# Pairing the short TensorE pieces of two recurrences in one decoder layer

## The chip, the core and the metric

The kernel is one program on one core of a Trainium2 chip. Its time is the device time of one launch, in microseconds (us). TensorE multiplies matrices; its matrix instructions come from one in-order stream. VectorE (DVE), ScalarE (ACT) and GpSimd (POOL) do the elementwise work, and SyncE (SP) issues most of the transfers. All five run their own in-order streams and wait for each other through semaphores.

## The reference, cut to what matters

One layer, batch 1, 512 tokens, width 1024, everything float32:

```
h = x + 1/2 * SwiGLU_1(RMSNorm(x))
h = h + HybridMixer(RMSNorm(h))
h = h + 1/2 * SwiGLU_2(RMSNorm(h))
y = RMSNorm_final(h)
```

The mixer projects the normed input to some 13,000 columns and uses them in two branches:

```
HGRN2, 8 heads:           S = diag(f_t) S + k_t^T v_t          o_t = S^T q_t
Gated DeltaNet, 16 heads: S = a_t (I - b_t k_t k_t^T) S + b_t k_t v_t^T   o_t = S^T q_t
y = sigmoid(gate_h) * (o_hgrn W_h) + sigmoid(gate_g) * (o_gdn W_g);   return y W_out
```

Both recurrences are computed in chunks; the second needs, for each chunk and head, the inverse of a unit triangular matrix.

## The kernel before

Activations lie feature by feature: 8 tiles of 128 partitions (features) by 512 tokens. Every dense product is done in three matmuls of rounded halves (`mm3`, L165 to L168: high by high, high by low, low by high), each 128x512. A row marked L166, L167 or L168 is one of these; three of them, a *triple*, are the smallest dense step. Weights come in slabs of 128x512 that SP loads (`raw`), ACT rounds (`whi`, L2179) and DVE subtracts (`wlo`, L2181).

The three stages follow each other: the first SwiGLU, the mixer, the second SwiGLU. In the mixer, dense products (`product`, L2201) and the two recurrences share TensorE. The recurrences use plain float32 matmuls in short pieces, each a few instructions long:

- HGRN2 (`h_head`, L1274): `pd` (L1289), seven levels of `pl` (L1326 on 128x32 tiles of the array, L1340 on smaller tiles), then `po` and `pu` by chunk (L1387 to L1392).
- Gated DeltaNet works on eight pairs of heads, u = 0 to 7, in four chunks of 128 tokens. Ahead of a recurrence stand `pgq` (L1592) and the triangular inverse with `pq1` to `pq4` (L1681 to L1712, on 32x32 and 64x64 tiles). The recurrence itself (`g_rec`, L1725) is a chain by chunk: `pks` (L1766, L1767) reads the state `s`; DVE makes `x` or `gx` from it (L1770); `pw` (L1779) reads that; DVE makes `we` or `gwe` (L1784) and ACT copies `w` or `gw` (L1736); `pog` (L1793, L1795) reads these; DVE makes the next `s` (L1806). That is 3 `pks`, 4 `pw` and 4 `pog` in each of eight recurrences, 88 pieces.

The order of all five engines in the mixer is fixed while the program is built, by a planner (`Desk`, L54). Each thread of work is a generator that asks for an engine for an assumed time: 0.69 us for a dense triple, 0.46 for `pw`, 0.88 for `pks`, 0.9 for `pog`, 0.65 or 0.6 for `pq1` to `pq4`. `run` (L107) repeatedly takes the engine that can start earliest and, on it, the thread of the lowest rank that is ready. Recurrences have ranks under 9, the dense products rank 9. So a short piece goes in front of the next triple as soon as it is ready, and ready means `SLACK` = 0.8 us after its inputs are planned to be done. The instructions are issued in the planned order; on the chip only that order is kept, and semaphores set the times.

Of the kernel before, what the change touches and what calls it, by code (L numbers as in the profile page):

```python
# [19 lines left out]
D = 1024  # L20
# [25 lines left out]
STAY = (15,)  # L46
CONVS = 6
SLACK = 0.8
LAG = dict(raw=3.5, gb=6.5, nb=6, m=7, out=5, back=6)
EASE = 2.5  # L50
LANES = {"a": 2, "b": 2, "d": 1, "e": 1}
# [2 lines left out]
class Desk:  # L54
# [5 lines left out]
    def __init__(self, **places):  # L60
        self.left, self.at, self.idle, self.now = dict(places), {}, {}, 0.0
        self.busy, self.asked, self.cur = [], [], None

    def start(self, rank, gen):
        th = type("Thread", (), {})()
        th.rank, th.gen, th.t = rank, gen, self.cur.t if self.cur else self.now
        self.resume(th)
# [39 lines left out]
    def run(self):  # L107
        self.settle()
        while self.busy:
            ready = {}  # L110
            for th in self.busy:
                e = th.want[1]
                r = th.t + (SLACK if e == "PE" and th.rank[0] < 9 else 0)
                ready.setdefault(e, []).append((r, th))
            t, e = min((max(self.idle.get(e, 0.0), min(r for r, _ in w)), e) for e, w in ready.items())
            th = min((th for r, th in ready[e] if r <= t), key=lambda th: th.want[3:] or th.rank)
            self.now = t
            self.idle[e] = th.t = t + th.want[2]
            self.busy.remove(th)
            self.resume(th)  # L120
            self.settle()
        assert not self.asked, [(th.rank, th.want) for th in self.asked]


def body(tc, xT, cst, sqc, hmask, dta, w1o, w1a, w2a, wm, wt, wn, wab, wbh, wbg, wo, w1b, w2b, yT, yN, dbg=None):
# [889 lines left out]
    with tc.tile_pool(name="mp", bufs=1) as mp:  # L1015
        mixer(tc, mp, locals())
# [7 lines left out]
def mixer(tc, mp, e):  # L1024
    nc = tc.nc
    pe, act, dve, pool, sp = nc.tensor, nc.scalar, nc.vector, nc.gpsimd, nc.sync
# [9 lines left out]
    def v3(ap, a):  # L1036
        return ap.rearrange("p (a b) -> p a b", a=a)
# [18 lines left out]
    for size, names in ((1024, "n2:2 gz:2 fs:1 ut:1"), (512, "kn:3 gm:1 qm:2 gb:2 ln:1 at:4 vb:4 t64:2 on:2"),  # L1056
                        (256, "ft:1 tp:1 thg:2 x:1 we:1 s:3 w:1"), (128, "fm:1"), (64, "sm:4")):
        for it in names.split():
            n, b = it.split(":")
# [39 lines left out]
    D = Desk(xt=0, zo=0, wx0=1, wx1=1, wx2=1, wx3=1, mm=2, a=2, b=2, d=1, e=1, ta=TA, tm=6, thg=1, raw=RB, w=WB, n2=2, gz=2, fs=1, ut=1, t=3, kn=3, gm=1,  # L1099
             qm=2, gb=2, ln=1, mi=3, mt=3, at=4, vb=4, t64=2, on=2, ft=1, x=1, we=1, w_=1, s=3)  # L1100
# [15 lines left out]
    def turned(x, src, mem, then=None, *arg, step=True):  # L1116
# [7 lines left out]
        sp.dma_start(mem, x)  # L1124
        yield "lag", LAG["out"]

# [9 lines left out]
    def regroup(to, mem):  # L1136
# [4 lines left out]
        else:  # L1141
            rows = mem.rearrange("(t s) (b c r) -> c (s b) t r", t=4, b=4, c=NT)
            for c in range(NT):
                yield "use", "SP", .5
                sp.dma_start(v3(to[:, c], 4), rows[c])
        yield "lag", LAG["back"]


    def decays(pab):
# [71 lines left out]
        sp.dma_start(gtd, gt)  # L1221
        yield "lag", LAG["out"]
        D.fire("decays")
# [284 lines left out]
    def g_e(u, st):  # L1508
# [3 lines left out]
        for i in range(2):  # L1512
# [4 lines left out]
            sp.dma_start(gb, gtd[hd_:hd_ + 1].rearrange("o (c b) -> o c b", c=NT).to_broadcast([P, NT, P]))  # L1517
            yield "lag", LAG["gb"]
            a = G["at"][u % 4 * 2 + i]
# [91 lines left out]
    def g_b(u, st):  # L1611
# [4 lines left out]
        for b in range(4):  # L1616
            r = slice(32 * b, 32 * b + 32)
            yield S
            sp.dma_start(nb[b].rearrange("s i j -> i s j"), n2[r, :, :, r].rearrange("p a c j -> p (a c) j"))
        yield "lag", LAG["nb"]  # L1620
        yield "on", *([("P", u - 2)] if u > 1 else [("m2", 0)] if u else ["m"])
# [9 lines left out]
        sp.dma_start(t, eye4)  # L1631
        yield "lag", LAG["m"]
        for j in range(31):
# [665 lines left out]
    def norm():  # L2299

        acc = e["acc"]
        yield "get", "d", 1
        yield "lag", 7.6
        yield T_(1.8)
        pt = ps("pst")
        for i in range(NT):
            c = slice(i * P, (i + 1) * P)
            pe.matmul(pt[:, i:i + 1], acc[:, c], ones[:, :1], start=True, stop=False)
            pe.matmul(pt[:, i:i + 1], rbc[:, c], ones[:, :1], start=False, stop=True)
        yield V(4)  # L2310
        v = rcols[:, 4:8]
        dve.tensor_scalar(v, pt[:, :4], 1.0 / (KD * P), EPS, op0=ALU.mult, op1=ALU.add)
        D.put("d")
        yield "use", "POOL", 1.2
        pool.tensor_tensor(rcol, v, mhalf[:, :4], op=ALU.pow)
        yield "get", "d", 1
        yield T_(.9)
        pb = ps("pbc")
        for i in range(NT):
            pe.matmul(pb[:, i * P:(i + 1) * P], rcol[:, i:i + 1].to_broadcast([P, P]), ident, start=True, stop=True)  # L2320
        yield A(512)
        act.copy(rbc, pb)
        D.put("d")
        D.fire("rbc")

    G["tp"] = [places["tp"]("gtp", (P, 8, 32))]
    D.start((0,), norm())
    D.start((3, -1), loader())
# [126 lines left out]
```

## Time and profile before

| | |
|---|---|
| median of 3 runs | 1584.68 us (1583.71 to 1585.51) |
| the profiled execution | 1584.17 us, span 1582.1 us |
| TensorE busy | 1574.2 us of the span |
| VectorE busy | 1095.0 us (69%) |
| ScalarE busy | 867.2 us (55%) |
| mean granted TensorE clock | 0.999 of full speed |
| first recurrence piece of DeltaNet (`pw`) | at 731.4 us of the span |
| last of them to start (`pw`, u = 7) | at 1085.3 us |

A row of the timeline gives the start from the span's beginning, the time that the merged instructions took, engine, line, operation, what was written from what, tile of the array and shape, and how many were merged. A float32 matmul of a short piece appears as two records. Starts of TensorE's instructions are recorded, ends are modelled and overlap the next start, so costs on TensorE are read from start to start.

### The profile page before, as it was taken

How to read it: one execution, taken by the hardware profiler on the slowest of the kernel's cores; microseconds unless marked ns; L12 is line 12 of the kernel's file. 1: busy time of each engine (PE TensorE's matmuls, PEld its weight loads, DVE VectorE, ACT ScalarE, POOL GpSimd, SP SyncE). 2: the span in 40 equal slices, each digit the busy share in tenths (PEclk: the TensorE clock that was granted, in tenths of full speed). 3: DMA queues.
4: the chain of work that ended last, by engine and by line, in shares of the span. 5: the costliest groups of instructions: out<-in, count | busy, mean ns of one | idle time of the engine just before them, and what ended most of it. 6: DMA issues, size and time to landing. Idle time of an engine off the chain costs nothing.

```text
span 1582.1 us, 28663 instructions
## 1 busy us (share of the span) xinstructions
PE 1574.2 (100%) x10344; PEld 1357.7 (86%) x10344; DVE 1095.0 (69%) x2027; ACT 867.2 (55%) x1891; POOL 382.9 (24%) x727
## 2 busy tenths in 40 slices
PE   9999999999999999999999999999999999999998
PEld 8999998888788788888888888888888899999887
DVE  5988884547778668758878776564555888888352
ACT  7776663334326335657576666554234766666232
POOL 0322200100222221074550566600001322220011
PEclk9999999999999999999999999999999999999999
DMA  6888843542323224565454765565645888873342
GB/s 218 180 205 184 186 100 88 181 122 91 101 68 95 72 80 138 163 211 174 127 167 129 224 193 157 185 202 159 205 155 171 219 185 186 186 169 95 90 137 90
DMA packets 172397, 240.66 MB, mean 152 GB/s; under 512 B 40272, under 2 KB 65488, under 8 KB 172256
## 3 DMA queue, kind: packets, MB, share of 16 engines
q1 hardware_dynamic: 155408, 208.55, 41.8%
q0 software_dynamic: 16416, 29.89, 12.3%
q8 instruction: 81, 1.33, 0.3%
q14 instruction: 60, 0.49, 0.1%
q10 hardware_dynamic: 432, 0.40, 0.1%
HBM read 208.07 MB, written 30.70 MB: 151 GB/s over the span
## 4 chain that ended last, share of the span: by engine, by line
PE 96%; issue 1%; DMA 1%; DVE 1%; SPq 0%; ACT 0%; POOL 0%; POOLq 0%; DVEq 0%; ACTq 0%
PE pmm L166 19%; PE pmm L168 18%; PE pmm L167 18%; PE pfa L475 3%; PE pfy L168 2%; PE pfx L167 2%; PE pfy L166 2%; PE pfx L168 2%; PE pfy L167 2%; PE pfx L166 2%; PE pnat L166 2%; PE pfa L167 2%; PE pfa L168 2%; PE pfa L166 2%; PE pnat L168 2%; PE pnat L167 2%
## 5 line engine op out<-in xcount | busy, mean ns | idle before, releaser
L166 PE MATMUL pmm<-uhl,whi 128*128 128x512 f32 x788 | 326.2, 414 | 0.1
L168 PE MATMUL pmm<-uhl,wlo 128*128 128x512 f32 x788 | 308.4, 391 | 0.3 <-DVE wlo L162 0.3
L167 PE MATMUL pmm<-uhl,whi 128*128 128x512 f32 x788 | 307.6, 390 | 0.0
L2179 ACT CAST whi<-raw 128x512 fp32r<-128x512 f32 x230 | 142.5, 620 | 235.7 <-PE pmm L167 184.7
L2181 DVE TENSOR_TENSOR wlo<-raw,whi 128x512 fp32r<-128x512 f32 x230 | 161.3, 704 | 144.1 <-ACT whi L2179 138.2
L168 PEld LDWEIGHTS pmm<-uhl,wlo 128*128 128x128 f32 x788 | 147.9, 188 | 33.2 <-DVE wlo L162 0.7
L166 PEld LDWEIGHTS pmm<-uhl,whi 128*128 128x128 f32 x788 | 148.2, 188 | 28.9 <-DVE fa L243 0.5
L167 PEld LDWEIGHTS pmm<-uhl,whi 128*128 128x128 f32 x788 | 148.5, 188 | 26.6
L166 PE MATMUL pmm<-gh,whi 128*128 128x512 f32 (+1 forms) x374 | 141.2, 377 | 0.0
L167 PE MATMUL pmm<-gl,whi 128*128 128x512 f32 (+1 forms) x374 | 140.8, 377 | 0.0
L168 PE MATMUL pmm<-gh,wlo 128*128 128x512 f32 (+1 forms) x374 | 140.8, 377 | 0.0
L439 DVE TENSOR_TENSOR sig<-h,sig 128x1024 fp32r<-128x1024 f32 x76 | 92.8, 1221 | 58.6 <-ACT sig L437 58.6
L437 ACT CAST sig<-h 128x1024 fp32r<-128x1024 f32 x76 | 79.8, 1050 | 94.0 <-PE pfx L168 33.5
L204 POOL TENSOR_TENSOR acc<-acc,sqt 128x512 f32<-128x512 f32 x18 | 24.1, 1341 | 373.5 <-ACT sqt L202 373.4
L606 DVE TENSOR_TENSOR wlo<-raw,whi 128x512 fp32r<-128x512 f32 (+1 forms) x80 | 55.5, 698 | 81.8 <-ACT whi L604 81.7
L604 ACT CAST whi<-raw 128x512 fp32r<-128x512 f32 (+1 forms) x80 | 46.9, 588 | 94.9 <-PE pmm L167 84.8
L407 POOL DMA_DIRECT2D wlo<-w1b x60 | 52.0, 868 | 140.8 <-ACT s L495 97.9
L168 PEld LDWEIGHTS pmm<-gh,wlo 128*128 128x128 f32 x374 | 70.4, 188 | 12.9
L166 PEld LDWEIGHTS pmm<-gh,whi 128*128 128x128 f32 x374 | 70.4, 188 | 12.9
L167 PEld LDWEIGHTS pmm<-gl,whi 128*128 128x128 f32 x374 | 70.4, 188 | 12.8
L1477 DVE SCALAR_TENSOR_TENSOR cy<-pmm,cs,cy 128x511 f32<-128x511 f32 (+2 forms) x96 | 71.6, 746 | 11.0 <-ACT cy L1474 8.7
L407 POOL DMA_DIRECT2D wlo<-w1a x54 | 46.8, 867 | 126.6 <-ACT s L495 85.9
(545 smaller groups left out, 4150.1 us busy)
## 6 DMA issues: line engine op xcount, KB each, us to landing
raw<-wt SPq DMA_DIRECT2D x152, 256.0 KB
raw<-w1b SPq DMA_DIRECT2D x80, 256.0 KB
raw<-w1a SPq DMA_DIRECT2D x72, 256.0 KB
wlo<-w1b POOLq DMA_DIRECT2D x60, 256.0 KB, 5.6
wlo<-w1a POOLq DMA_DIRECT2D x54, 256.0 KB, 6.2
raw<-w2a SPq DMA_DIRECT2D x40, 256.0 KB
raw<-w2b SPq DMA_DIRECT2D x40, 256.0 KB
raw<-wn SPq DMA_DIRECT2D x32, 256.0 KB
```

What stands on the lines that cost most here:

```text
L166: pe.matmul(pt, ah, bh, start=first, stop=False, **kw)
L167: pe.matmul(pt, ah, bl, start=False, stop=False, **kw)
L168: pe.matmul(pt, al, bh, start=False, stop=last, **kw)
L407: pool.dma_start(lo, src_, accum_op=ALU.add)
L437: act.copy(hl[:, 0:2], s)
L439: dve.tensor_tensor(hl[:, 2:4], s, hl[:, 0:2].bitcast(F32), op=ALU.subtract)
L475: pe.matmul(pa.rearrange("p (x t) -> p x t", x=2), hi[:, w], x, start=first and p == 0, stop=False, skip_group_check=True)
L604: act.copy(hi[:, :n], raw[:, :n])
L606: dve.tensor_tensor(lo[:, :n], raw[:, :n], hi[:, :n].bitcast(F32), op=ALU.subtract)
L1477: dve.scalar_tensor_tensor(y[:, j:], pt[:, :T - j], wc[3 - j], y[:, j:], op0=ALU.mult, op1=ALU.add)
L2179: act.copy(hi, raw)
L2181: dve.tensor_tensor(lo, raw, hi.bitcast(F32), op=ALU.subtract)
```

## The change

The planner gets two rules, both switched on in the mixer alone (`D.paired = PAIRED`).

The first holds short pieces. While the plan's clock is between 400 and 700 us, and a dense triple stands at TensorE as well, a short piece is not placed until a second one is ready, or until the first has been ready for 8 us. The rule applies only when the last thing placed on TensorE was dense, so once a piece has been placed others may follow at once.

The second charges TensorE for a change of kind: 0.03 us is added to a short piece that follows dense work, 0.115 us to a triple that follows a short piece. This holds through the whole mixer and shifts the plan's clock for all engines.

No instruction is added or taken away; the order on the five engines changes.

```diff
@@ -46,6 +46,9 @@
 STAY = (15,)
 CONVS = 6
 SLACK = 0.8
+PAIRED = 2
+WHEN = ((400, 700, 8.0),)
+TURN = 0.03, 0.115
 LAG = dict(raw=3.5, gb=6.5, nb=6, m=7, out=5, back=6)
@@ -60,6 +63,7 @@
     def __init__(self, **places):
         self.left, self.at, self.idle, self.now = dict(places), {}, {}, 0.0
         self.busy, self.asked, self.cur = [], [], None
+        self.paired, self.short = 0.0, False
@@ -107,15 +111,24 @@
     def run(self):
         self.settle()
         while self.busy:
-            ready = {}
+            ready, held = {}, 0.0
+            wait = max([v for a, b, v in WHEN if a <= self.now < b], default=0.0) if self.paired and not self.short else 0.0
+            if wait:
+                pe = [th for th in self.busy if th.want[1] == "PE"]
+                ts = sorted(th.t for th in pe if th.rank[0] < 9)
+                if ts and len(ts) < len(pe):
+                    held = min(ts[PAIRED - 1] if ts[PAIRED - 1:] else ts[0] + wait, ts[0] + wait)
             for th in self.busy:
                 e = th.want[1]
-                r = th.t + (SLACK if e == "PE" and th.rank[0] < 9 else 0)
+                r = max(th.t, held) + SLACK if e == "PE" and th.rank[0] < 9 else th.t
                 ready.setdefault(e, []).append((r, th))
             t, e = min((max(self.idle.get(e, 0.0), min(r for r, _ in w)), e) for e, w in ready.items())
             th = min((th for r, th in ready[e] if r <= t), key=lambda th: th.want[3:] or th.rank)
             self.now = t
             self.idle[e] = th.t = t + th.want[2]
+            if e == "PE" and self.paired and (th.rank[0] < 9) != self.short:
+                self.idle[e] = th.t = th.t + TURN[self.short]
+                self.short = not self.short
             self.busy.remove(th)
@@ -2323,6 +2336,7 @@
         D.fire("rbc")
 
+    D.paired = PAIRED
     G["tp"] = [places["tp"]("gtp", (P, 8, 32))]
```

Lines of this part of the program stand 13 lower after the change, so L166 becomes L179 and L1793 becomes L1806.

Two places of TensorE's order show what moves. The first is in the middle of the DeltaNet part: in the kernel before, from one `pog` to the `pks` that reads its new state (`s_8592`). `pq3` is a piece of another pair's inverse.

```order
L1793 MATMUL pog_8588<-gwe_6494,gkn_6077 128x256
L1795 MATMUL pog_8588<-gw_6555,gat_6218 128x128
L1795 MATMUL pog_8588<-gw_6555,gat_6219 128x128
L166 MATMUL pmm_8506<-uhl_71,whi_8349 128x512
L167 MATMUL pmm_8506<-uhl_71,whi_8349 128x512
L168 MATMUL pmm_8506<-uhl_71,wlo_8348 128x512
L1704 MATMUL pq3_8606<-h_70,gn2_7245 64x64 x8
L166 MATMUL pmm_8623<-uhl_71,whi_8358 128x512
L167 MATMUL pmm_8623<-uhl_71,whi_8358 128x512
L168 MATMUL pmm_8623<-uhl_71,wlo_8357 128x512
L1766 MATMUL pks_8635<-s_8592,h_70 128x256
L1767 MATMUL pks_8635<-s_8592,h_70 128x256
```

The same step of the same recurrence on TensorE after the change (the state is `s_8582` here, and `pq4` is the next piece of that inverse):

```order
L1806 MATMUL pog_8578<-gwe_6527,gkn_6096 128x256
L1808 MATMUL pog_8578<-gw_6455,gat_6238 128x128
L1808 MATMUL pog_8578<-gw_6455,gat_6239 128x128
L1725 MATMUL pq4_8589<-acc_72,gt64_7184 64x64 x8
L179 MATMUL pmm_8555<-uhl_71,whi_8352 128x512
L180 MATMUL pmm_8555<-uhl_71,whi_8352 128x512
L181 MATMUL pmm_8555<-uhl_71,wlo_8351 128x512
L179 MATMUL pmm_8555<-uhl_71,whi_8352 128x512
L180 MATMUL pmm_8555<-uhl_71,whi_8352 128x512
L181 MATMUL pmm_8555<-uhl_71,wlo_8351 128x512
L1779 MATMUL pks_8621<-s_8582,h_70 128x256
L1780 MATMUL pks_8621<-s_8582,h_70 128x256
```

The small-tile piece has moved from between two triples to directly behind `pog`; two triples and one small piece lie between `pog` and `pks` in both.

The second place is later on TensorE, from a `pks` to the `pw` that follows it in its chain. Before the change (pair u = 6):

```order
L1766 MATMUL pks_12059<-s_12025,h_70 128x256
L1767 MATMUL pks_12059<-s_12025,h_70 128x256
L166 MATMUL pmm_12009<-uhl_71,whi_11808 128x512
L167 MATMUL pmm_12009<-uhl_71,whi_11808 128x512
L168 MATMUL pmm_12009<-uhl_71,wlo_11807 128x512
L166 MATMUL pmm_12009<-uhl_71,whi_11808 128x512
L167 MATMUL pmm_12009<-uhl_71,whi_11808 128x512
L168 MATMUL pmm_12009<-uhl_71,wlo_11807 128x512
L166 MATMUL pmm_12009<-uhl_71,whi_11808 128x512
L167 MATMUL pmm_12009<-uhl_71,whi_11808 128x512
L168 MATMUL pmm_12009<-uhl_71,wlo_11807 128x512
L1779 MATMUL pw_12082<-gx_6461,gut_6341 128x128 x2
```

And at about the same count of dense triples after it (pair u = 5, which is still running there):

```order
L1779 MATMUL pks_11948<-s_11912,h_70 128x256
L1780 MATMUL pks_11948<-s_11912,h_70 128x256
L1725 MATMUL pq4_11955<-acc_72,gt64_6952 64x64 x8
L179 MATMUL pmm_11868<-uhl_71,whi_11664 128x512
L180 MATMUL pmm_11868<-uhl_71,whi_11664 128x512
L181 MATMUL pmm_11868<-uhl_71,wlo_11663 128x512
L179 MATMUL pmm_11975<-uhl_71,whi_11715 128x512
L180 MATMUL pmm_11975<-uhl_71,whi_11715 128x512
L181 MATMUL pmm_11975<-uhl_71,wlo_11714 128x512
L1792 MATMUL pw_11987<-x7_7613,x5_7637 128x128 x2
```

Between `pks` and `pw` stood three triples; now a small-tile piece joined to `pks` and two triples stand there.

## Rows read from the trace of the kernel before

**Rows 1.** The page, part 1: busy time, share, instructions of each engine.

```profile
PE 1574.2 (100%) x10344; PEld 1357.7 (86%) x10344; DVE 1095.0 (69%) x2027; ACT 867.2 (55%) x1891; POOL 382.9 (24%) x727
```

**Rows 2.** Timeline of TensorE around one `pw` that stands alone.

```profile
740.44 0.39 PE L166 MATMUL pmm<-uhl,whi 128*128 128x512 f32 x1
...
740.89 0.39 PE L168 MATMUL pmm<-uhl,wlo 128*128 128x512 f32 x1
741.12 0.60 PE L1779 MATMUL pw<-gx,gut 128*128 128x128 f32 x4
741.48 0.48 PE L166 MATMUL pmm<-uhl,whi 128*128 128x512 f32 x1
741.79 0.40 PE L167 MATMUL pmm<-uhl,whi 128*128 128x512 f32 x1
```

**Rows 3.** Timeline of TensorE around two `pw` in a row.

```profile
763.17 0.39 PE L168 MATMUL pmm<-uhl,wlo 128*128 128x512 f32 x1
763.40 0.60 PE L1779 MATMUL pw<-gx,gut 128*128 128x128 f32 x4
763.84 0.61 PE L1779 MATMUL pw<-gvb,h 128*128 128x128 f32 x4
...
764.52 0.40 PE L167 MATMUL pmm<-uhl,whi 128*128 128x512 f32 x1
```

**Rows 4.** Timeline of TensorE around one `pq2` alone.

```profile
752.61 0.39 PE L168 MATMUL pmm<-uhl,wlo 128*128 128x512 f32 x1
752.92 0.69 PE L1691 MATMUL pq<-acc,x 32*32 32x32 f32 x32
...
753.88 0.40 PE L167 MATMUL pmm<-uhl,whi 128*128 128x512 f32 x1
```

**Rows 5.** Timeline of TensorE around one `pgq` alone.

```profile
714.42 0.39 PE L168 MATMUL pmm<-uhl,wlo 128*128 128x512 f32 x1
714.65 1.02 PE L1592 MATMUL pgq<-h 128*128 128x256 f32 x4
...
715.74 0.40 PE L167 MATMUL pmm<-uhl,whi 128*128 128x512 f32 x1
```

**Rows 6.** Timeline of TensorE around `pq2` and `pgq` in a row.

```profile
929.49 0.39 PE L168 MATMUL pmm<-uhl,wlo 128*128 128x512 f32 x1
929.80 0.69 PE L1691 MATMUL pq<-acc,gtp 32*32 32x32 f32 x32
930.43 1.13 PE L1592 MATMUL pgq<-h 128*128 128x256 f32 x4
...
931.62 0.40 PE L167 MATMUL pmm<-uhl,whi 128*128 128x512 f32 x1
```

**Rows 7.** Timeline of TensorE around one `pl` on 128x32 tiles.

```profile
395.47 0.39 PE L168 MATMUL pnat<-whi,uhl 128*128 128x512 f32 x1
395.79 0.45 PE L1326 MATMUL pl<-qp,ke 128*32 128x16 f32 x32
...
396.50 0.39 PE L167 MATMUL pnat<-wlo,uhl 128*128 128x512 f32 x1
```

**Rows 8.** Timeline of TensorE around two such `pl` in a row.

```profile
577.54 0.39 PE L168 MATMUL pnat<-whi,uhl 128*128 128x512 f32 x1
577.86 0.74 PE L1326 MATMUL pl<-qp,ke 128*32 128x16 f32 x64
...
578.86 0.39 PE L167 MATMUL pnat<-wlo,uhl 128*128 128x512 f32 x1
```

**Rows 9.** Waits of TensorE, 380 to 1145 us: total, times, longest.

```profile
PE pks L1766 <- DVE s L1806: 0.2, 1, 0.2
```

**Rows 10.** Timeline of all engines: links of one chain, 736 to 744 us.

```profile
737.24 0.59 PE L1767 MATMUL pks<-s,h 128*128 128x256 f32 x2
...
739.59 0.35 DVE L1770 SCALAR_TENSOR_TENSOR gx<-pks,sm,gvb 128x128 f32<-128x128 f32 x1
...
742.50 0.61 DVE L1784 TENSOR_SCALAR gwe<-pw,gx 128x128 f32<-128x128 f32 x2
...
743.62 0.59 PE L1793 MATMUL pog<-gwe,gkn 128*128 128x256 f32 x2
```

## The prediction

> **What bounds the kernel now.** I read the busy shares of the page first: TensorE is busy for 1574.2 of 1582.1 us, and the next engine, VectorE, for 1095.0 [rows 1]. So TensorE's stream sets the time, and only two things can move it: the work in that stream becomes shorter, or TensorE has to wait. Then I read the waits of TensorE over the mixer: the view names one, 0.2 us long [rows 9]. There is nothing to win back from waits in that stretch. What remains is the cost of TensorE's own pieces, and for that I read the timeline of TensorE from start to start, at places where a short piece stands alone between dense matmuls and at places where the old order happened to put two in a row. The reader is to see in these rows what a second piece adds behind a first.
>
> **The change part by part.** Counted in the order that TensorE gets, the mixer has 196 unbroken stretches of short pieces before and 165 after, with the same instructions. So 31 times a change from dense work to short pieces and back disappears, nearly all in the DeltaNet part. The question is what one such change costs.
>
> Dense matmuls start 0.225 us apart (740.44 to 740.89 is two of them) [rows 2]. Around a lone `pw` it takes 0.90 us from the last dense start ahead of it (740.89) to the second dense start behind it (741.79); without the piece it would be two pitches, 0.45. So the lone `pw` costs 0.45 us, both changes of kind included [rows 2]. Two `pw` in a row: 763.17 to 764.52 is 1.35, less 0.45 is 0.90 us [rows 3], twice the lone one. The second piece saved nothing. The same for pieces of unlike shape: `pq2` alone costs 1.27 - 0.45 = 0.82 us [rows 4], `pgq` alone 1.32 - 0.45 = 0.87 [rows 5], the two in a row 2.13 - 0.45 = 1.68 [rows 6], against a sum of 1.69. A join is worth 0.00 to 0.01 us.
>
> Why it looks dearer is also in [rows 2]: the first dense start behind the piece is followed by the next only 0.31 us later, 0.09 more than the pitch. But that dense matmul itself had started 0.36 us after `pw`, where four records at the 0.11 us that one costs (0.45 over 4) ask for 0.44. The extra behind the piece is the piece's own tail, which the records put into the next pitch. It is not a toll that a join avoids. I take 0.005 us a join, so 31 x 0.005 = 0.2 us less; the two ends are 0 and 31 x 0.01 = 0.3.
>
> There is one kind of join that does pay. A lone `pl` on 128x32 tiles costs 1.03 - 0.45 = 0.58 us [rows 7], two in a row 1.32 - 0.45 = 0.87 [rows 8], 0.29 less than 2 x 0.58. Here both pieces use a small tile of the array, and one entry into it and exit from it is spared. The order counts four such neighbours of `pl` pieces before and three after, since the shifted plan also reorders the HGRN2 part. That is one join lost, 0.3 us more. The joins that the change makes are of another kind: a full-array piece (`pks`, `pw`, `pog`, `pgq`) beside another or beside a small-tile `pq`. Changes of tile shape in the stream number 158 before and 159 after.
>
> The Trainium skill has a rule that fits this (TensorEngine Tiling (Array Packing), Key Properties): changing the tiling mode, not merely the tile, drains the TensorE. By that rule a stretch of full-array pieces spares no drain when joined, and a full-array piece beside a small-tile one leaves both changes of mode where they were, so the rule speaks against a gain from these joins. [Rows 6] agree (0.01 us for a mixed join) and so do [rows 7, 8] (0.29 us where one visit to the small tile is spared); by the rule alone, with 159 changes of mode for 158, the sum would be a shade above no change.
>
> Next, waits. Nothing else hides behind TensorE: on the other engines the instructions are the same, and VectorE, the busiest, has 31% of idle time over the span [rows 1]. But the order fixes how many triples stand between two links of a chain, and the new charge of 0.145 us a stretch (0.03 + 0.115) is time that the planner sees and the chip does not: its old charge of 0.46 for `pw` already covers the 0.45 measured. With 165 stretches the plan now counts 165 x 0.145 = 24 us of TensorE work that, for full-array pieces, doesn't exist. So links are planned with more time than they will have. How much is there to lose? The second `gx` starts at 739.59 and takes 0.35, so it is done at 739.94, and `pw` starts at 741.12: 1.2 us spare. `gwe` is done at 743.11 and `pog` starts at 743.62: 0.5 us spare [rows 2, 10]. One or two stretches between links take 0.15 to 0.3 us of this. Most links keep something. At the two places shown in the section on the change, the distance is about what it was: `pog` to `pks` has two triples and one small piece in both, `pks` to `pw` had 3 x 0.675 = 2.0 us and now has 2 x 0.675 + 0.82 = 2.2. A held piece also has more spare time, not less, since its inputs were ready before it was let go.
>
> If a link does run dry, what waits behind it is TensorE's whole stream, the dense triples included, so each such wait is paid in full. The trace of before can't show how many there will be. Bounds: none (the 0.2 us of [rows 9] gone as well), or a third of the 88 chain pieces, 29, each late by 0.25 us (between the 0.15 and 0.3 above, rounded up), 7 us. I take 0.5 us more than now, two or three short waits, because the spare times in [rows 2, 10] are above the erosion.
>
> The transfers and weight slabs: SP's and ACT's orders shift with the plan, but the dense triples keep their count, and slabs are made several triples ahead; I cost this at nothing, hidden by the slabs that stand ready, and if that cover went, the wait would be one conversion late, under 1 us a time.
>
> Sum, against the profiled execution's 1584.17 us (span 1582.1): -0.2 for joins, +0.3 for the lost neighbour, +0.5 for waits, 1584.8. The median of the runs is 0.5 above the profiled execution, so I forecast 1585.3 us. By bounds, the forecast's own range is from 1584.68 - 0.3 - 0.2 = 1584.2 to about 1588, a handful of waits short of the 7 us.
>
> **The rivals.**
>
> Faster: a change of kind really costs what the planner charges, 0.145 us. Then 31 x 0.145 = 4.5 us go, 1580.2 us. For it: dense after short starts 0.31 apart instead of 0.225 [rows 2]. Against it: the doubled and the mixed pieces, which should then be 0.145 below their sum and are 0.00 and 0.01 below it [rows 3, 6]. Chance 0.06.
>
> Slower, by links that run dry: the 24 us that only the plan sees come off the spare time of the DeltaNet chains, and TensorE stops in front of `pks`, `pw` or `pog`. Price at the upper bound 7 us, 1592 us; it decides from about 13 late links of 0.25 us, 3.2 us. For it: the spare time at `pog` is only 0.5 us [rows 10]. Against it: one wait so far in 88 pieces [rows 9], and a held pair has more spare time. Chance 0.12.
>
> Slower, at the end: holding delays the recurrences, and the branch product that needs their last heads waits. The last `pog` stands 11 triples ahead of that product in the order before and 5 after, 6 x 0.675 = 4 us later, 1589 us if it all shows. Against it: the last two heads are read 50 triples after the product starts, some 34 us, and their transposes still stand 21 triples (14 us) ahead of that. Chance 0.04.
>
> That the change doesn't join pieces is excluded by the order: 31 stretches fewer.
>
> **How the numbers follow.** 0.2% is 3.2 us, about what a measurement of this kernel can tell from no change, so no change means 1581.5 to 1587.9. The forecast has 0.78: it lies inside, but its upper end touches 1588, and I count 0.01 of it as slower. Faster is the first rival less the case that it comes out half as large: 0.05, and 0.01 of it stays within. Slower: 0.12 less 0.01 for a mild form, plus 0.04 and the 0.01 above, 0.16. Within: 0.79. The range from 1582.3 to 1589.0 leaves out the faster rival and the heavy end of the first slower one, together near 0.15.
>
> **What would show it.** In the profile after: a `pw` or `pks` joined to another full-array piece still costs its lone 0.45 or 0.87 us from start to start; TensorE stays near 1574 us busy; TensorE's waits in the mixer total under 2 us. I am wrong if joined pieces come out 0.1 us or more below their sum (then 1580), or if waits on `s`, `gx`, `gwe` or `gw` add up to several us in front of chain pieces, or a wait of some us stands where the branch product reads its last heads.

## The result, and the profile after

The changed kernel takes 1587.37 us (median of 21 runs, 1586.74 to 1589.05) against 1584.68 us (21 runs, 1583.67 to 1586.51). The ratio is 1.0018, 95% interval 1.0012 to 1.0024: 2.7 us slower, inside the 0.2% that I had called no change, and above the 1585.3 us forecast. The profiled execution took 1588.55 us, 4.4 us more than that of before, so the sizes below are those of one execution at the slow edge.

The first line of the page after, which answers to [rows 1] (busy time, share, instructions):

```profile
PE 1575.9 (99%) x10344; PEld 1358.7 (86%) x10344; DVE 1093.6 (69%) x2027; ACT 867.1 (55%) x1891; POOL 385.0 (24%) x727
```

TensorE is as busy as it was, within 1.7 us, while the span grew from 1582.1 to 1586.6 us: the pieces did not become cheaper, and waits came. The waits of TensorE over the mixer, which answer to [rows 9] (total, times, longest):

```profile
PE po L1402 <- DVE hs L1411: 0.7, 1, 0.7
PE pq L1725 <- POOL fm L1650: 0.5, 1, 0.5
PE pd L1302 <- DVE qq L1297: 0.5, 1, 0.5
PE pmm L179 <- DVE cy L1490: 0.5, 2, 0.3
PE pmm L180 <- DVE oh L1463: 0.2, 1, 0.2
PE po L1402 <- DVE hs L1409: 0.2, 1, 0.2
```

That is 2.6 us in six kinds of waits where one wait of 0.2 us stood. Four of the six (`po` twice, `pd`, and the products that read `oh`) belong to the HGRN2 part, where nothing is held and only the charge for a change of kind acts. None of the named waits is at `pks`, `pw` or `pog`. The view leaves out shorter ones: read from start to start, two lone `pog` cost 1.14 us in place of 0.88 (at 1034.23 and 1063.89 us), as before the change two `pks` were late by 0.46 and 0.32 us (at 801.53 and 956.92 us).

All kernels here run the same number of dense triples, so the start of the triple with the same number can be compared; by the 1000th, all kernels of the table have the same short pieces behind them. The differences from before, in us, of the last row (L168 or its successor) of the 650th triple (mixer begins), the 1000th (HGRN2 done), the 1470th and 1600th (before and after the recurrences' last heads are read) and the 2350th (last):

| kernel | 650 | 1000 | 1470 | 1600 | 2350 |
|---|---|---|---|---|---|
| the change | 0.35 | 3.68 | 3.95 | 4.48 | 4.48 |
| charge_only | 0.49 | 3.82 | 12.62 | 12.62 | 12.62 |
| hold_only | 0.46 | 0.44 | -4.52 | 3.48 | 3.48 |
| charge_early | 0.05 | 3.64 | 8.10 | 8.62 | 8.62 |
| charge_late_hold | 0.04 | 0.07 | -1.53 | 4.05 | 4.05 |

A negative number means that fewer short pieces than before are done at that triple. Of the 4.1 us that the changed kernel loses in the mixer, 3.3 are lost by the 1000th triple, and 0.8 in the DeltaNet part.

**The joined pieces.** TensorE's timeline after the change, at a `pw` joined to a `pog`, and at a `pog` joined to a `pq4`; these answer to [rows 2 to 6]:

```profile
860.05 0.40 PE L181 MATMUL pmm<-uhl,wlo 128*128 128x512 f32 x1
860.28 0.61 PE L1792 MATMUL pw<-gx,x 128*128 128x128 f32 x4
860.73 0.60 PE L1806 MATMUL pog<-x,x 128*128 128x256 f32 x2
...
861.84 0.39 PE L180 MATMUL pmm<-uhl,whi 128*128 128x512 f32 x1
```

```profile
852.23 0.39 PE L181 MATMUL pmm<-uhl,wlo 128*128 128x512 f32 x1
852.45 0.59 PE L1806 MATMUL pog<-gwe,gkn 128*128 128x256 f32 x2
...
853.42 0.68 PE L1725 MATMUL pq<-acc,gt 64*64 64x64 f32 x16
...
854.37 0.39 PE L180 MATMUL pmm<-uhl,whi 128*128 128x512 f32 x1
```

Less two dense pitches (0.45), the first stretch costs 861.84 - 860.05 - 0.45 = 1.34 us. A lone `pog` costs 0.88 from start to start (20 of them in the trace of before agree), a lone `pw` 0.45: their sum is 1.33. The second stretch costs 854.37 - 852.23 - 0.45 = 1.69; `pog` 0.88 and `pq4` 0.82 make 1.70. Over all 44 joined stretches of the DeltaNet part in this trace, with 55 joins in them, the cost is 0.42 us below the sum of the lone pieces, 0.008 us a join (0.3 to 0.5 us, as the dense pitch is taken as 0.227 or 0.225 us). Before, that part had 26 joins. So the change earned 29 x 0.008 = 0.2 us.

**One wait, followed back.** `pd` starts 496.64 - 495.74 = 0.90 us after the triple ahead of it, 0.7 more than the pitch. All engines' timeline there, with the steps that led to it:

```profile
493.54 1.28 ACT L1252 ACT_TABLE_LOAD   x1
...
494.84 0.60 ACT L1252 ACTIVATE qq<-pmm 128x512 f32<-128x512 f32 x1
...
495.47 0.69 DVE L1294 TENSOR_TENSOR qp<-qq,f 128x512 f32<-128x512 f32 x1 [1.22 <-ACT qq L1252]
...
495.74 0.40 PE L181 MATMUL pmm<-uhl,wlo 128*128 128x512 f32 x1
496.20 0.29 DVE L1297 COPY qq<-qp 128x256 f32<-128x256 f32 x1
...
496.64 0.56 PE L1302 MATMUL pd<-qq,ke 128*128 128x192 f32 x2 [0.50 <-DVE qq L1297]
```

ScalarE first loads a table for the new function, 1.28 us, which the planner does not count (its assumed time for this activation is 0.66 us). Before, such a load stood there as well, but `pd` came 3.2 us after its `qq`; now it comes 1.2 us after. These 2.0 us are far more than the 0.15 to 0.3 us that the prediction had the charge take from a link. The `po` at 507 us has the same form on VectorE:

```profile
504.68 1.14 DVE L1466 SCALAR_TENSOR_TENSOR oh<-xo,cs,oh 128x128 fp32r<-128x128 f32 x4 [1.00 <-ACT oh L1460]
...
504.95 0.39 PE L1405 MATMUL pu<-v,hkn 128*128 128x128 f32 x2
...
505.83 0.95 DVE L1345 COPY_PREDICATED ah<-hm,pl 32x64 f32<-32x64 int32 x3
...
506.81 0.42 DVE L1365 TENSOR_TENSOR qp<-qp,fl 128x256 f32<-128x256 f32 x1
507.27 0.35 DVE L1411 SCALAR_TENSOR_TENSOR hs<-hs,fl,pu 128x128 f32<-128x128 f32 x1
...
507.68 0.49 PE L1402 MATMUL po<-hs,qp 128*128 128x128 f32 x2 [0.73 <-DVE hs L1411]
```

VectorE was held for 1.0 us by ScalarE's `oh`, then worked off what stood ahead of `hs`; `hs` needs the `pu` of 504.95 and older values, so it could have run when `oh` was done, 1.5 us earlier. From start to start the stretch with this `pd` costs 0.7 us more than a lone one and the stretch with this `po` 1.0 us more than its pieces did before. Both stand with the same cost in charge_only and charge_early, the runs below that share the order of this part: the waits come with the order, and not by chance of one execution.

### The profile page after: what moved, and what is told of

Its sections match the earlier page's. It is cut to its first block, busy times and chain, and to the rows that moved or that the text cites. A ratio compares the mean times of both kernels' runs of the same rounds, so it can differ in the third digit from the quotient of the medians.

```text
span 1586.6 us, 28669 instructions
## 1 busy us (share of the span) xinstructions
PE 1575.9 (99%) x10344; PEld 1358.7 (86%) x10344; DVE 1093.6 (69%) x2027; ACT 867.1 (55%) x1891; POOL 385.0 (24%) x727
## 3 DMA queue, kind: packets, MB, share of 16 engines
q8 instruction: 81, 1.33, 0.3%
## 4 chain that ended last, share of the span: by engine, by line
PE 56%; issue 1%; DVE 1%; DMA 1%; POOL 1%; ACT 0%; POOLq 0%; DVEq 0%; SPq 0%; ACTq 0%
PE pmm L179 13%; PE pmm L180 12%; PE pmm L181 12%; PE pfa L488 2%; PE pfy L181 1%; PE pfx L180 1%; PE pfy L179 1%; PE pfx L181 1%; PE pfy L180 1%; PE pfx L179 1%; PE pfa L181 1%; PE pfa L180 1%; PE pfa L179 1%; PE pgq L1605 1%; PE pog L1808 1%
## 5 line engine op out<-in xcount | busy, mean ns | idle before, releaser
L179 PE MATMUL pmm<-uhl,whi 128*128 128x512 f32 x788 | 321.9, 408 | 0.6 <-DVE cy L1490 0.5
L179 PEld LDWEIGHTS pmm<-uhl,whi 128*128 128x128 f32 x788 | 148.1, 188 | 31.1 <-issue 1.3
L179 PE MATMUL pmm<-gh,whi 128*128 128x512 f32 (+1 forms) x374 | 141.2, 377 | 0.0
L179 PEld LDWEIGHTS pmm<-gh,whi 128*128 128x128 f32 x374 | 70.4, 188 | 12.7
```

Source lines behind the costliest of these rows:

```text
L179: pe.matmul(pt, ah, bh, start=first, stop=False, **kw)
```

## The experiments

Three theories stood at the start. **A**: a join is worth nothing to speak of; what was lost came from the new order of the HGRN2 stretch, which the charge brings. **B**: holding costs the time, the charge is harmless. **C**: a change of kind costs 0.145 us, as the planner now has it, and the gain was lost elsewhere. All ratios are to the kernel before on the same chip.

**charge_only.** The charge without holding.

```diff
-WHEN = ((400, 700, 8.0),)
+WHEN = ()
```

> The charge for a change of kind through the whole mixer, nothing held: 201 stretches of short pieces (196 before, 165 in the changed kernel); TensorE's order up to the first DeltaNet piece is that of the changed kernel. Theory A (a join is worth nothing, the loss comes from the new order of the HGRN2 stretch that the charge brings): 3 us or so lost by the end of HGRN2 as in the changed kernel, time 1587.5, between 1586.5 and 1589. Theory B (holding costs the time, the charge is harmless): 1584.7. Theory C (a change of kind costs 0.145 us, and the changed kernel loses elsewhere what its joins win): 36 stretches more than the changed kernel, 5.2 us above it, 1592.5.

Measured: 1596.55 us, ratio 1.0074 (1.0061 to 1.0086), 11.6 us slower. By the 1000th triple it has lost 3.3 us, as the changed kernel has: A holds there, B falls. But A put the whole time at 1589 at most, and 8.8 us more go in the DeltaNet part. C's 1592.5 is nearer, but not for C's reason: the 18 undisturbed joins of this trace took 0.004 us off each. Two of TensorE's waits there, and what VectorE and ScalarE did ahead of the first:

```profile
PE pq L1725 <- ACT acc L1719: 3.0, 1, 3.0
PE pmm L179 <- DVE cy L1490: 1.3, 1, 1.3
```

```profile
967.34 0.75 DVE L1944 SCALAR_TENSOR_TENSOR og<-og,cs,zo 128x512 f32<-128x512 f32 x1 [1.86 <-DMA og<-od]
...
968.17 0.62 ACT L1953 CAST soat<-og 128x512 fp32r<-128x512 f32 x1 [6.97 <-DVE og L1944]
968.69 0.61 ACT L2192 CAST whi<-raw 128x512 fp32r<-128x512 f32 x1
969.33 0.37 ACT L1719 COPY acc<-pq 128x256 f32<-128x256 f32 x1
```

ScalarE sat for 7 us before an operand of the branch product that was not due for long, and the copy that `pq4` needed was queued behind it. The operand is made from VectorE's `og`, which had itself waited for a transfer (`od`), so this stop goes back to a transfer that landed late for the planned order. Behind the stop TensorE's granted clock fell. The windows of TensorE in the same run (busy time and count, granted clock, DMA share, GB/s):

```profile
960.00:966.00 6.00, 6.00 (x46) 1.00 0.92 297
966.00:969.60 3.60, 0.79 (x4) 0.90 0.68 232
969.60:976.00 6.40, 6.25 (x29) 0.52 0.67 153
976.00:982.00 6.00, 6.00 (x32) 1.00 0.45 142
```

After the 3 us without work the granted clock is 0.52 of full speed, the 1.2 GHz level for most of the stretch; dense starts are 0.43 us apart there, in place of 0.225, for eleven matmuls. The stop is 3.1 us from start to start (969.75 - 966.40, less a pitch of 0.225); `pq4` itself then took 0.6 us more than a lone one, and the eleven dense matmuls 11 x 0.2 = 2.3 us more, 6.0 us in all. Of the other 2.8 us, 1.5 are the wait of a product on `cy` (774.37 - 772.65, less a pitch) and 0.7 a late `pks` at 918 us.

**hold_only.** Holding without the charge.

```diff
-TURN = 0.03, 0.115
+TURN = 0.0, 0.0
```

> Holding as in the change, charge set to zero: 170 stretches, HGRN2 order as in the kernel before, the last recurrence piece 33 triples later than before. Theory A: 1584.7, between 1583.5 and 1586, with HGRN2 to the tenth as before, and joined pieces that cost their sum. Theory B: 1587 or more. Theory C: 26 stretches fewer x 0.145 = 3.8 us less, 1580.9.

Measured: 1587.87 us, ratio 1.0021 (1.0011 to 1.0030). Nothing is lost by the 1000th triple, as A had it, but the whole is 1.9 us above A's upper end, and B's "1587 or more" is met, though not by what the changed kernel loses up to the 1000th triple. TensorE's timeline where the branch product reads the last heads:

```profile
1130.00 0.39 PE L181 MATMUL pmm<-uhl,wlo 128*128 128x512 f32 x1
...
1131.19 0.50 PE L179 MATMUL pmm<-uhl,whi 128*128 128x512 f32 x1 [0.36 <-ACT uhl L1870]
...
1133.23 0.49 PE L179 MATMUL pmm<-uhl,whi 128*128 128x512 f32 x1 [0.58 <-ACT uhl L1870]
1133.96 0.50 PE L180 MATMUL pmm<-uhl,whi 128*128 128x512 f32 x1 [0.23 <-DVE uhl L1872]
...
1134.53 0.39 PE L179 MATMUL pmm<-uhl,whi 128*128 128x512 f32 x1
```

From 1130.00 to 1134.53 are 4.53 us for seven dense pitches (1.58) and one `pto`, a transpose of the last heads (0.45): 2.5 us are lost. The last recurrence piece stands 33 triples later than before. So holding by itself has a price here, at the end of the mixer: the third rival of the prediction, in this order but not in the changed kernel's. C's 1580.9 is excluded: the joins here took 0.005 us off each.

**charge_early.** The charge in the HGRN2 stretch alone, nothing held.

```diff
-WHEN = ((400, 700, 8.0),)
+WHEN = ()
...
-                self.idle[e] = th.t = th.t + TURN[self.short]
+                self.idle[e] = th.t = th.t + TURN[self.short] * (t < 380)
```

> The charge only in the first 380 us of the plan, that is in the HGRN2 stretch, nothing held: 202 stretches. Theory A: all of the loss of the changed kernel is there, 1587.5, between 1586.5 and 1589. Theory B: 1584.7. Theory C: 6 stretches more than before, 1585.6.

Measured: 1590.63 us, ratio 1.0038 (1.0025 to 1.0050). The 1000th triple is 3.6 us late, so the charge in that stretch suffices for the changed kernel's loss there. The DeltaNet part, which carries no charge of its own here, loses 5 us more, and the time is above A's range: the shifted start alone gave it another order, with waits of 1.2 and 1.6 us, start to start, of products for a buffer (on `cy`), 0.4 us ahead of a `pq2`, and 1.6 us for eight dense matmuls at the lower clock behind them (granted 0.51 from 823.8 to 827.0 us).

**slack_075.** The kernel before with another small shift.

```diff
-SLACK = 0.8
+SLACK = 0.75
```

> The kernel before with SLACK 0.75 in place of 0.8, no charge, nothing held: another small shift of the same plan, 203 stretches. Theory A1 (any shift of the plan away from the order of before costs some us in HGRN2, through waits of 0.2 to 1 us at single pieces): 1586 to 1589. Theory A2 (the charge itself is what harms, since it gives links too little time): within 1 us of 1584.7. Theory C: 7 stretches more, 1585.7.

Measured: 1589.44 us, ratio 1.0027 (1.0017 to 1.0037). A2 put this within 1 us of 1584.7 and falls: a shift without any charge costs as much. A1 is nearer, its upper end 0.4 us below the result, but in place of its several short waits there is one long one, of a kind that the changed kernel has at 0.2 us (`oh`), and again the clock behind it (granted 0.51 from 646.7 to 650.2 us):

```profile
643.82 0.60 PE L1435 MATMUL pt<-sq,hon 128*128 128x128 f32 x4
646.69 0.79 PE L166 MATMUL pmm<-oh,whi 128*128 128x512 f32 x1 [2.28 <-ACT oh L1447]
647.47 0.79 PE L167 MATMUL pmm<-oh,whi 128*128 128x512 f32 x1
```

**charge_late_hold.** The change, with the charge after 380 us of the plan alone, so that HGRN2 keeps its order.

```diff
-                self.idle[e] = th.t = th.t + TURN[self.short]
+                self.idle[e] = th.t = th.t + TURN[self.short] * (t >= 380)
```

> The change with the charge only after 380 us of the plan, so in the DeltaNet part alone; holding as in the change. HGRN2 order as in the kernel before; 170 stretches; the last recurrence piece 31 triples later than before, 1496 against 1465. Theory A: nothing lost by the end of HGRN2, and joined pieces that cost their sum; waits at the end of the mixer as in the run with holding alone (2 to 3 us there), time 1587 to 1588.5. If the 3.3 us lost in HGRN2 belonged to the change as such and not to the charge's shift of that stretch, they would stand here too: 1590 or more. Theory C (0.145 us a change): 26 stretches fewer, 1581 plus waits.

Measured: 1587.71 us, ratio 1.0016 (1.0007 to 1.0025). HGRN2 loses nothing (0.07 us at the 1000th triple), so its 3.3 us belong to the charge in that stretch. The total is within A's range, but not for A's reason: of the waits only the last and shortest is at the end. TensorE's waits:

```profile
PE pog L1808 <- ACT x L1749: 1.3, 1, 1.3
PE pks L1779 <- DVE s L1819: 0.9, 1, 0.9
PE pog L1806 <- DVE gwe L1797: 0.8, 1, 0.8
PE pog L1808 <- ACT gw L1749: 0.5, 1, 0.5
PE pmm L180 <- DVE uhl L1872: 0.3, 1, 0.3
```

These are links of the DeltaNet chain that ran dry, the prediction's first slower rival. At the first of them all engines' timeline shows why:

```profile
1015.82 1.57 ACT L1840 ACTIVATE gat<-gat,sm 128x128 f32<-128x128 f32 x5
...
1017.30 0.60 ACT L2192 CAST whi<-raw 128x512 fp32r<-128x512 f32 x1
...
1017.80 0.98 ACT L1840 ACTIVATE gat<-gat,sm 128x128 f32<-128x128 f32 x3
...
1018.69 0.35 ACT L1749 COPY x<-pw 128x256 f32<-128x256 f32 x1
...
1019.10 0.60 PE L1808 MATMUL pog<-x,gat 128*128 128x128 f32 x3 [1.29 <-ACT x L1749]
```

The copy of `pw` stands behind eight activations of another recurrence and a weight slab. So this link ran dry by ScalarE's order; that the charge ate its spare time, as the rival had it, is not shown.

**hold_hgrn.** Holding in the HGRN2 stretch, no charge.

```diff
-WHEN = ((400, 700, 8.0),)
-TURN = 0.03, 0.115
+WHEN = ((0, 340, 8.0),)
+TURN = 0.0, 0.0
```

> Holding in the HGRN2 stretch (first 340 us of the plan) in place of the DeltaNet one, no charge: 144 stretches against 196, and now 27 neighbours of pl pieces against 4, 106 changes of tile shape against 155. Theory A with the small-tile price: a full-array join is worth under 0.01 us, a join that spares a visit to a small tile 0.2 to 0.3 us, so 25 visits fewer take 5 to 7 us off the cost of HGRN2's pieces; since the recurrences end 56 triples later than before, the end of the mixer waits and the time is above 1590 all the same. Theory C: every stretch counts alike, 52 fewer x 0.145 = 7.5 us off, and the full-array joins show 0.145 each. Rival (holding costs nothing at the end): 1579.

Measured: 1692.68 us, ratio 1.0676 (1.0657 to 1.0695). The late HGRN2 heads are the likely cause, which was not followed further (TensorE's longest wait is 7.7 us, the clock's mean 0.962). It still shows which joins pay. Two `pl` of one tile shape in a row, the counterpart of [rows 8]:

```profile
418.21 0.39 PE L181 MATMUL pmm<-uhl,wlo 128*128 128x512 f32 x1
418.52 0.74 PE L1339 MATMUL pl<-qp,ke 128*32 128x16 f32 x64
...
419.53 0.39 PE L180 MATMUL pmm<-uhl,whi 128*128 128x512 f32 x1
```

1.32 - 0.45 = 0.87 us, 0.29 under two lone ones, and at every undisturbed pair of that shape in this run the saving is 0.24 to 0.29 us. The joins of full-array pieces took 0.006 us off each. So C falls once more, and the small-tile price stands.

**change_slack_095.** The change, with slack that gives the charge back.

```diff
-SLACK = 0.8
+SLACK = 0.95
```

> The changed kernel with SLACK 0.95 in place of 0.8, which gives each short piece back the 0.145 us that the charge takes. If the waits in HGRN2 come from spare time that the charge ate (A2), they go: TensorE's waits up to the end of HGRN2 under 0.5 us, 2.5 us less than in the changed kernel there. If they come from any shift of a plan that had been settled at one order (A1), waits of like size stand at other pieces. The whole is slower in both, since the recurrences end 55 triples later than before: 1590 to 1600.

Measured: 1601.57 us, ratio 1.0102 (1.0089 to 1.0116). By the 1000th triple it has lost 3.9 us, no less than the changed kernel (3.3), and TensorE's two waits for `oh` there alone are 1.8 us where A2 allowed 0.5: A2, that the waits come from spare time eaten by the charge, falls again. This order is a new one as well, so the links of the changed kernel themselves are not tested by it. Most of the rest is the late end of the recurrences (one wait of 5.7 us for the last heads' operand, with the lower clock behind it), and the whole is 1.6 us above the expected range.

**measured_costs.** The kernel before, with the planner's costs of small-tile pieces as the trace has them (the last two edits each in two places).

```diff
-                yield T_(.6 if hh <= 16 else .5)
+                yield T_(.58 if hh <= 32 else .82)
...
-            yield T_(.65)
+            yield T_(.83)
...
-            yield T_(.6)
+            yield T_(.82)
```

> The kernel before, no charge and nothing held, with the planner's costs of small-tile pieces set to what the trace shows: 0.83 for pq1 and pq2 (was 0.65), 0.82 for pq3 and pq4 (was 0.6), 0.58 and 0.82 for pl (was 0.6 and 0.5). 205 stretches. If waits come from wrong costs in the plan, a truer plan has fewer: 1583.5 to 1584.5. If any shift costs (A1): 1586 to 1590. Theory C: 9 stretches more, 1586.

Measured: 1586.98 us, ratio 1.0013 (1.0004 to 1.0022). A truer cost of TensorE's pieces did not give fewer waits. A1 holds, with a smaller loss than in the other shifts.

**hold_shorter.** Holding without the charge, for less time.

```diff
-WHEN = ((400, 700, 8.0),)
-TURN = 0.03, 0.115
+WHEN = ((400, 650, 3.0),)
+TURN = 0.0, 0.0
```

> Holding without the charge, but only to 650 us of the plan and for 3 us at most: 179 stretches (170 with the full hold, 196 before), last recurrence piece 20 triples later than before in place of 33. HGRN2 order as before. Theory A: the 2.6 us of waits that the run with holding alone had where the end of the mixer reads the last heads are gone or under 0.5 us, joins give 0.1 us, so 1584.5 to 1586 unless chain pieces in the DeltaNet part now wait. Theory C: 17 stretches fewer x 0.145 = 2.5 us less, 1582.5. If the waits at the end came from elsewhere than the late recurrence, 1587.5.

Measured: 1585.40 us, ratio 1.0002 (0.9993 to 1.0011), as A had it. TensorE's one named wait over the mixer:

```profile
PE pw L1792 <- DVE x L1783: 0.4, 1, 0.4
```

The waits at the end are gone with the earlier end of the recurrences. With 17 stretches fewer and no waits to speak of, the time is that of before: joining is worth nothing here, neither way. None of the nine orders tried is faster than that of before.

## Why the prediction was right or wrong

- **TensorE sets the time, and only its work or its waits can move it**: right. Its busy time moved by 1.7 us, the rest is waits.
- **A join is worth 0.00 to 0.01 us, 0.2 us in all**: right, 0.008 us over 55 joins, and 0.003 to 0.007 in the experiments. The faster rival (0.145 us a change) is excluded by each of them; hold_shorter is the plainest.
- **One small-tile neighbour lost, +0.3 us**: the price was right (0.29 us again in hold_hgrn), the sum was not. The four joins of before save 0.21, 0.21, 0.29 and 0.21, those after 0.21, 0.31 and 0.29, so 0.1 us was lost.
- **+0.5 us for waits**: this is the step that was mis-sized. Named waits rose from 0.2 to 2.6 us, and from start to start the mixer lost 4.1 us in the profiled execution, where the medians of the whole kernel differ by 2.7. The prediction's own sign, waits under 2 us in the mixer, was missed. I put the waits at the DeltaNet chain, where pieces are held; they stood mostly in HGRN2. I had called that part reordered and then priced only its `pl` neighbours. What charge_early and charge_late_hold show is that the charge in that stretch alone makes this loss.
- **The mechanism for waits, that the charge takes 0.15 to 0.3 us off the spare time of each link**: not borne out as the cause in HGRN2. Giving the 0.145 us back (change_slack_095) left the loss as it was, and a shift without a charge (slack_075) made one as large. What the followed waits have in common is that another instruction stood in front in an in-order stream: a table load, a wait for another thread's operand, activations of another recurrence. That the order of before happens to have few such meetings is a reading of its 0.2 us of named waits; the planner does not see some of their costs, the table load among them. That each of the waits has this form was followed for four (`pd`, `po`, `pq4` in charge_only, `pog` in charge_late_hold), not for all.
- **Links run dry in the DeltaNet part**: hardly in the changed kernel (two `pog` 0.26 us late each), yes in charge_late_hold, 3.5 us of named waits.
- **Late recurrences at the end**: not in the changed kernel (5 triples ahead sufficed, as argued), yes in hold_only, where the end came 33 triples later.
- **Range and forecast**: 1587.37 lies within 1582.3 to 1589.0 and within 0.2%; the move was up, and by waits, as forecast, but at five times their forecast size, mostly in another part and not by the mechanism given. That the sum still fell inside is partly luck: the same charge without the holding (charge_only) took 1596.55 us.

What stays open is why the order of charge_only has these stops in the DeltaNet part, 8.8 us with the clock behind them, and that of the changed kernel, with the same charge and the holding, loses only 0.8: the two orders differ in too many places to name one.

## What to carry to other kernels

Before joining pieces to spare a change, find two that already stand together in the trace and compare them, start to start, with the lone ones; the longer pitch behind a piece is its own tail. A rule or a cost in a planner that fixes the order of five in-order streams moves everything behind it, so it has to be priced as a new draw of all the waits, also in stretches that it was not meant for, and against a kernel whose order was already good none of the ten draws here (the changed kernel and nine more) was better. A join paid here where both pieces use small tiles of the array: 0.29 us for two of the same shape, 0.21 for 128x32 beside 128x64.

## What the runs showed of the hardware

A stop of TensorE can be paid nearly twice, since the granted clock may fall to its lower level, 1.2 GHz, behind it. In charge_only a stop of 3.1 us was followed by 4.3 us of dense starts 0.43 us apart (971.39 to 975.66), and 2.9 us more were paid. In slack_075 a stop of 2.5 us was followed by 2.7 us of starts 0.40 to 0.60 us apart (647.47 to 650.17), and 1.8 us more were paid. In charge_early the clock fell 2.4 us after a stop of 1.6 us had ended, and in change_slack_095 behind two stops of 1.0 and 1.2 us with one matmul between them (granted 0.50 from 639.2 to 642.5 us). A single stop of 1.5 us in charge_only (772.65 to 774.37) left it at 1.00, and so did the waits of the changed kernel, 0.9 us from start to start at most. So the length of one stop did not decide it alone. The Trainium skill (TensorE: Matmul & The Clock Gate, HAM oscillation — how this bites in real kernels) says that a wait between two bursts of matmuls can throttle TensorE again, so that the next burst starts cold; charge_only and slack_075 agree, with 2.9 us paid behind the 3.1 us stop.

A visit of TensorE to the 128x32 tiles of the array costs about 0.29 us beside the work itself (0.58 us for one `pl`, 0.87 for two in a row), the same in the HGRN2 part of before and in hold_hgrn.

A change between the dense matmuls and short float32 pieces of the full array costs nothing that can be read here: 0.00 to 0.01 us a join, over the 55 joins of the changed kernel.
